# A two-engine weight-sum pipeline in the down projection of a hybrid decoder layer: two of four block sums formed on VectorE, dead storage reused, steps in another order

## The chip, the cores and the metric

One Trainium2 (trn2) chip, one of its cores. The metric is the device time of one execution of the whole program in microseconds (us), as the median of several runs. The profiled execution has a trace of its own; every instruction time below comes from it.

## The reference

The kernel computes one decoder layer on 256 tokens behind 16 prepended meta tokens, 2048 features wide, in float32. All that matters here is the last part, the gated feed-forward block with a causal convolution over three tokens:

```python
u = rmsnorm(h, norm_ffn)
up = causal_dwconv(u @ w_up, ffn_conv_w, ffn_conv_b)
gate, val = jnp.split(up, [FFN_DIM], axis=-1)      # FFN_DIM = 5632
h = h + (jax.nn.silu(gate) * val) @ w_down         # w_down: 5632 x 2048
h = rmsnorm(h, norm_final)                         # the last 256 rows are the output
```

Ahead of it stand the input projection, eight retention heads, four mLSTM heads and the output projection, which the change does not touch.

## The kernel before, in words

All products are made in float32 precision out of a faster format (`F32R`): each operand x is split into hi = x rounded to that format and lo = x - hi, and a product is hi*hi + hi*lo + lo*hi, three matmuls. A weight tile arrives by DMA in a home called `wraw` (four homes, also used by all other weights), ScalarE copies it to `whi` (five homes), VectorE subtracts to give `wlo` (five homes), and TensorE multiplies. A weight tile is 128 x 1024 floats, 512 KB.

The feed-forward block runs in two halves of the 5632 features. In each half an up phase computes 22 tiles of gate and value (`conv3`, silu, product) and stores the results split, and a down phase multiplies them with the half's rows of `w_down` and adds to the residual `hn` (two token blocks `tt` of 128 rows, 2048 columns). The first half is `half` 0, the second `half` 1. A helper `norm2` in the first up phase uses a scratch tile `tb` as well, and so do the sums of activations in the up phase (L720 to L724).

The down phase goes over two pairs of column blocks of 512, `b` = 0 and 2, so the pair is (b, b + 1). For each it walks 11 steps `q` of 256 features (two rows of blocks of 128):

- An even step (`PLAIN`) loads the two weight tiles of the pair with `load_step` and calls `product` for both token blocks: 24 matmuls of 512 columns.
- An odd step (`FAST`, function `seven`) treats 2 token blocks x 2 feature blocks times 2 feature blocks x 2 column blocks as a 2 x 2 product made with seven block products in place of eight: 21 matmuls. It needs the weight tiles `raw0` and `raw1` themselves and four sums of their blocks: GpSimd (POOL in the profile) forms them, two in `ta`, two in `tb`, in a chain: ta1 = raw1[1] - raw1[0], tb0 = ta1 + raw0[0], ta0 = raw1[0] - raw0[0], tb1 = raw0[1] - tb0 (L757). `raw0` uses a `wraw` home; `raw1`, `ta` and `tb` have one home each. Each of the four is then split (L696 on ScalarE, L697 on VectorE) and multiplied (L771, L772, L775), in the order raw0, raw1, ta, tb: 6, 3, 6 and 6 matmuls.

Four accumulators `cs[tt, j]` (PSUM name `atps`) hold what belongs to one output block, four others `ps` (`mmps`) what several output blocks share. After the last odd step `share` folds the shared ones into `hn` with one ScalarE copy and eight VectorE additions, keeping its running sum in the first half of `ta` (L780). After the last step `add` (L798) adds each `cs` to `hn`. In half 1 `squares` (ScalarE) and `times_gain` (POOL, L644) follow at once on each finished block for the final norm. The very last column block, 3, has its even steps in a tail behind the loop of the last pair, with two token blocks staggered by `lag` = 4 steps, so that `finish` of token block 0 lies beside the last matmuls.

Each engine has a queue that runs in the order in which the compiler's scheduler wrote it; the scheduler goes by program order among what it believes to be ready. SyncE (SP) issues the weight loads from one queue, in order. `hT` is the residual in transposed form, 128 x 16 x 272 floats; its last readers are the transposes (L622) that fill `hn` in the first up phase, after which it is dead but keeps its home to the end.

Of the kernel before, what the change touches and what calls it, by code (L numbers as in the profile page):

```python
# [10 lines left out]
F32 = mybir.dt.float32  # L11
# [5 lines left out]
P = 128  # L17
# [66 lines left out]
def trunk(ctx: ExitStack, tc: tile.TileContext, io, out: bass.AP):  # L84
    nc = tc.nc

    def pool(name, bufs, **kw):
        return tc.tile_pool(name=name, bufs=bufs, **kw)
# [515 lines left out]
    def norm2():  # L604
        ms2 = at.tile([P, 512], F32, name="atps")
        nc.tensor.matmul(ms2[:, :NQ], inv_dm, ssq, start=True, stop=True)
        r0, rt = midp.tile([P, 2, 512], F32, name="tb").rearrange("p a t -> a p t")
        r = rsqrt_m2(r0, rt, ms2[:, :NQ], NQ, squared)
        nc.vector.tensor_scalar(out=rstd2, in0=r[:, :NQ], scalar1=-0.5, scalar2=None, op0=ALU.mult)

# [75 lines left out]
    FAST = list(range(1, NQD, 2))  # L686
    PLAIN = list(range(0, NQD, 2))
    S1, S2, S3, S4, A11, A12, A22 = range(7)
    for half in range(2):
        mh = midp.tile([P, 2 * len(PLAIN), SEQ], F32R, name="mh")  # L690
        ml = midp.tile([P, 2 * len(PLAIN), SEQ], F32R, name="ml")
# [7 lines left out]
        for jj in range(NHF):  # L699
            j = half * NHF + jj  # L700
            pair = []
            for s in range(2):
                pair.append(project(io["wu"][2 * j + s], uh, ul, 0))
                if j == 0 and s == 0:
                    norm2()
            gt = conv3(pair[0], j, "gt")
            vt = conv3(pair[1], NF + j, "vt")
            nc.scalar.activation(gt, gt, AF.Silu)
            nc.vector.tensor_tensor(out=gt, in0=gt, in1=vt, op=ALU.mult)
            q, i = divmod(jj, 2)  # L710
            if q in PLAIN:
                k = 2 * PLAIN.index(q) + i
                copied, parted = split(mh[:, k, :], ml[:, k, :], gt)
            elif i == 0:
                f = FAST.index(q)
                even = gt
                copied, parted = split(sh[:, f, A11, :], sl[:, f, A11, :], gt[:, 0:P])
            else:
                a11, a21, a12, a22 = even[:, 0:P], even[:, P:], gt[:, 0:P], gt[:, P:]
                sums = midp.tile([P, 2, 512], F32, name="tb")[:, 0, :].rearrange("p (a t) -> p a t", a=4)  # L720
                nc.gpsimd.tensor_tensor(out=sums[:, S1, :], in0=a21, in1=a22, op=ALU.add)
                nc.gpsimd.tensor_tensor(out=sums[:, S3, :], in0=a11, in1=a21, op=ALU.subtract)  # L722
                nc.gpsimd.tensor_tensor(out=sums[:, S2, :], in0=sums[:, S1, :], in1=a11, op=ALU.subtract)
                nc.gpsimd.tensor_tensor(out=sums[:, S4, :], in0=a12, in1=sums[:, S2, :], op=ALU.subtract)  # L724
                split(sh[:, f, A12:, :], sl[:, f, A12:, :], gt.rearrange("p (a t) -> p a t", a=2))
                copied, parted = split(sh[:, f, 0:4, :], sl[:, f, 0:4, :], sums)
            if 2 <= j < 18:
                with tc.issue_after(parted.ins):
                    transposed_h((j - 2) // 4, (j - 2) % 4)
# [12 lines left out]
            for i in range(2):  # L742
                nc.tensor.matmul(ps, mh[:, k + i, rows], lo[:, i, cols], start=False, stop=last and i == 1)  # L743

        def seven(w0, w1, q, cs, ps, fresh):

            f = FAST.index(q)
            raw0 = wpool.tile([P, 2, 512], F32, name="wraw", bufs=4)
            nc.sync.dma_start(raw0, w0)
            raw1 = midp.tile([P, 2, 512], F32, name="raw1")  # L750
            nc.sync.dma_start(raw1, w1)

            ta, tb = (midp.tile([P, 2, 512], F32, name=n) for n in ("ta", "tb"))
            sums = ((ta, 1, raw1[:, 1, :], raw1[:, 0, :], ALU.subtract), (tb, 0, ta[:, 1, :], raw0[:, 0, :], ALU.add),
                    (ta, 0, raw1[:, 0, :], raw0[:, 0, :], ALU.subtract), (tb, 1, raw0[:, 1, :], tb[:, 0, :], ALU.subtract))
            for t, i, a, b, op in sums:
                nc.gpsimd.tensor_tensor(out=t[:, i, :], in0=a, in1=b, op=op)  # L757
            first, last = q == FAST[0], q == FAST[-1]
            for w, to in (
                (raw0, ((A11, ps[0], first, last), (A12, cs[0, 0], False, False))),  # L760
                (raw1, (None, (S4, cs[0, 1], first and fresh, False))),
                (ta, ((S1, ps[1], first, last), (S3, ps[2], first, last))),
                (tb, ((S2, ps[3], first, last), (A22, cs[1, 0], False, False))),
            ):
                hi = wpool.tile([P, 2, 512], F32R, name="whi", bufs=5)
                lo = wpool.tile([P, 2, 512], F32R, name="wlo", bufs=5)
                a = 1 if to[0] is None else 0
                split(hi[:, a:, :], lo[:, a:, :], w[:, a:, :])
                for i in range(a, 2):
                    m, o, begin, _ = to[i]  # L770
                    nc.tensor.matmul(o, sh[:, f, m, :], hi[:, i, :], start=begin, stop=False)  # L771
                    nc.tensor.matmul(o, sl[:, f, m, :], hi[:, i, :], start=False, stop=False)  # L772
                for i in range(a, 2):
                    m, o, _, end = to[i]
                    nc.tensor.matmul(o, sh[:, f, m, :], lo[:, i, :], start=False, stop=end)  # L775

        def share(ps, b):

            p1, p5, p7, p6 = ps
            x = midp.tile([P, 2, 512], F32, name="ta")[:, 0, :]  # L780
            h = lambda tt, j: hn[:, tt, (b + j) * 512 : (b + j + 1) * 512]

            def plus(o, a, c):
                nc.vector.tensor_tensor(out=o, in0=a, in1=c, op=ALU.add)

            nc.scalar.copy(x, p1)
            plus(h(0, 0), p1, h(0, 0))
            plus(x, p6, x)
            plus(h(0, 1), p5, h(0, 1))
            plus(h(0, 1), x, h(0, 1))  # L790
            plus(x, p7, x)
            plus(h(1, 0), x, h(1, 0))
            plus(x, p5, x)
            plus(h(1, 1), x, h(1, 1))

        def add(ps, tt, c0):
            h = hn[:, tt, c0 : c0 + ps.shape[1]]
            nc.vector.tensor_tensor(out=h, in0=ps, in1=h, op=ALU.add)  # L798

        if half == 1:  # L800
            wk2_cm.__exit__(None, None, None)
            up_cm.__exit__(None, None, None)
            more_cm = pool("more", 3, side="right")
            more = more_cm.__enter__()
            gfin = more.tile([P, DM], F32, name="gfin", bufs=1)
            nc.gpsimd.dma_start(gfin, io["gfin"])
            junk = more.tile([P, 512], F32, name="junk", bufs=1)

        def load_step(b, q, to=wpool):
            return load_w(io["wd"][b, half * NQD + q], [P, 2, 512], to)  # L810

        for b in (0, 2):
            cs = {}
            for j in range(2):
                for tt in range(2):
                    cs[tt, j] = at.tile([P, 512], F32, name="atps")
            ps = [mm.tile([P, 512], F32, name="mmps") for _ in range(4)]

            final = half == 1 and b == 2
            for q in range(NQD):  # L820
                if q in FAST:
                    seven(io["wd"][b, half * NQD + q], io["wd"][b + 1, half * NQD + q], q, cs, ps, final)
                    if q == FAST[-1]:
                        share(ps, b)
                    continue
                for j in range(1 if final else 2):
                    w = load_step(b + j, q)
                    for tt in range(2):
                        product(cs[tt, j], tt, q, w, q == PLAIN[0], q == PLAIN[-1])
            for j in range(1 if final else 2):  # L830
                for tt in range(2):
                    c = (b + j) * 512
                    add(cs[tt, j], tt, c)
                    if half == 1:
                        squares(tt, b + j, c, c + 512)
                        times_gain(tt, c, c + 512)


        if half == 1:
            lag = 4  # L840
            c = 3 * 512
            ws = {}
            for n, q in enumerate(PLAIN):
                ws[q] = load_step(3, q, more if n % 2 else wpool)
                product(cs[0, 1], 0, q, ws[q], False, q == PLAIN[-1])
                if n >= lag:
                    q = PLAIN[n - lag]
                    product(cs[1, 1], 1, q, ws.pop(q), q == PLAIN[0], q == PLAIN[-1 - lag])
            add(cs[0, 1], 0, c)
            squares(0, 3, c, DM)  # L850
            gather(0, 3)
# [96 lines left out]
```

## Time and profile before

| what | us |
|---|---|
| median of three runs | 1245.96 (1245.83 to 1246.23) |
| the profiled execution | 1246.28 |
| its span, first to last instruction | 1244.5 |
| TensorE busy | 1217.1 (98%) |
| VectorE busy | 943.1 (76%) |
| ScalarE busy | 690.1 (55%) |
| POOL busy | 233.6 (19%) |
| first down phase, from its first to its last matmul | 720.66 to 845.30 |
| second down phase, first pair | 1099.44 to 1157.80 |
| second down phase, last pair with the tail | 1157.80 to 1236.05 |

The 1.8 us between the profiled execution and its span lie around the first and the last instruction. Matmuls overlap in their records, so the pace of TensorE is read from start to start, not from the durations. DVE is VectorE, ACT is ScalarE, PE is TensorE, PEld its weight loads, SP is SyncE. An entry `ta<-raw` is an instruction that writes a tile `ta` and reads `raw`; `raw` there is `raw1`, as the digits of names are left out.

### The profile page before, as it was taken

The numbers are of one execution on the slowest core, as the hardware profiler recorded it, in microseconds if no ns is written. First come the engines' busy times: TensorE is split into PE (matmuls) and PEld (weight loads), VectorE is DVE, ScalarE is ACT, GpSimd is POOL, SyncE is SP. The second block draws the span as 40 slices with busy tenths as digits, with TensorE's granted clock in tenths as the row PEclk, the third lists the DMA queues.
The fourth block names the chain that finished last, engine by engine and source line by source line (L and its number), as shares of the span: only waits on it lengthen the run. The fifth ranks groups of instructions, "written<-read, shape, count | busy, mean of one in ns | idle before, by whom it ended". The sixth has DMA issues, their size and how long they took to land.

```text
span 1244.5 us, 22568 instructions
## 1 busy us (share of the span) xinstructions
PE 1217.1 (98%) x8974; PEld 1160.6 (93%) x8974; DVE 943.1 (76%) x1349; ACT 690.1 (55%) x933; POOL 233.6 (19%) x183
## 2 busy tenths in 40 slices
PE   9999999999999999999999999899999999999787
PEld 9999999999999999999999987679999999988566
DVE  8877778677666667888888786879777777787776
ACT  8747655665557556555555545445555555554443
POOL 0100000111001110000100254460100100136661
PEclk9999999999999999999999999999999999999798
DMA  7765555655664655555555545557655555555343
GB/s 273 268 204 168 173 185 171 200 164 185 190 190 150 199 182 199 184 184 177 185 186 180 177 153 183 167 178 249 188 185 176 183 186 185 182 188 172 120 154 134
DMA packets 73290, 228.91 MB, mean 184 GB/s; under 512 B 13408, under 2 KB 17632, under 8 KB 73056
## 3 DMA queue, kind: packets, MB, share of 16 engines
q1 hardware_dynamic: 71952, 223.85, 54.9%
q0 software_dynamic: 656, 2.76, 0.7%
q8 instruction: 70, 1.15, 0.4%
q10 hardware_dynamic: 576, 0.85, 0.2%
q14 instruction: 36, 0.29, 0.1%
HBM read 222.98 MB, written 4.46 MB: 183 GB/s over the span
## 4 chain that ended last, share of the span: by engine, by line
PE 89%; POOL 3%; DVE 3%; DMA 2%; issue 2%; ACT 1%; SPq 0%; DVEq 0%; POOLq 0%; ACTq 0%
PE mmps L137 25%; PE mmps L140 25%; PE mmps L138 25%; PE atps L740 2%; PE atps L741 2%; PE atps L743 2%; POOL tb L757 2%; DMA raw<-in_wd 2%; DVE wlo L697 1%; POOL ta L757 1%; PE mmps L771 1%; PE mmps L775 1%; PE mmps L772 1%; PE atps L775 1%; PE atps L772 1%
## 5 line engine op out<-in xcount | busy, mean ns | idle before, releaser
L128 ACT CAST whi<-wraw 128x1024 fp32r<-128x1024 f32 x364 | 380.5, 1050 | 340.9 <-PE mmps L138 249.4
L130 DVE TENSOR_TENSOR wlo<-wraw,whi 128x1024 fp32r<-128x1024 f32 x364 | 461.5, 1271 | 71.1 <-ACT whi L128 66.9
L138 PE MATMUL mmps<-ul,whi 128*128 128x258 f32 x1408 | 345.8, 283 | 0.0
L137 PE MATMUL mmps<-uh,whi 128*128 128x258 f32 x1408 | 345.5, 282 | 0.0
L137 PEld LDWEIGHTS mmps<-uh,whi 128*128 128x128 f32 x1408 | 266.1, 189 | 0.1
L138 PEld LDWEIGHTS mmps<-ul,whi 128*128 128x128 f32 x1408 | 265.1, 188 | 0.1
L137 PE MATMUL mmps<-xh,whi 128*128 128x272 f32 (+2 forms) x864 | 220.2, 288 | 0.0
L138 PE MATMUL mmps<-xl,whi 128*128 128x272 f32 (+2 forms) x864 | 218.9, 286 | 0.0
L140 PE MATMUL mmps<-uh,wlo 128*128 128x258 f32 x1408 | 198.9, 284 | 0.0
L140 PEld LDWEIGHTS mmps<-uh,wlo 128*128 128x128 f32 x1408 | 182.4, 189 | 0.0
L137 PEld LDWEIGHTS mmps<-xh,whi 128*128 128x128 f32 x864 | 162.9, 189 | 0.1
L138 PEld LDWEIGHTS mmps<-xl,whi 128*128 128x128 f32 x864 | 162.6, 188 | 0.0
L140 PE MATMUL mmps<-xh,wlo 128*128 128x272 f32 (+2 forms) x864 | 127.1, 286 | 0.0
L140 PEld LDWEIGHTS mmps<-xh,wlo 128*128 128x128 f32 x864 | 114.7, 188 | 0.0
L626 DVE TENSOR_TENSOR cu<-mmps,rstd 128x258 f32<-128x258 f32 x88 | 37.5, 426 | 84.7 <-PE mmps L140 84.3
L740 PE MATMUL atps<-whi,mh 128*128 128x512 f32 (+1 forms) x200 | 78.9, 396 | 1.2 <-DVE hn L798 1.2
L741 PE MATMUL atps<-whi,ml 128*128 128x512 f32 (+1 forms) x200 | 78.2, 393 | 0.0
L722 POOL TENSOR_TENSOR tb<-gt 128x128 f32<-128x128 f32 x10 | 14.0, 1403 | 312.0 <-ACT whi L128 282.1
L138 PE MATMUL mmps<-mixl,whi 128*128 128x258 f32 x256 | 63.1, 283 | 0.0
L137 PE MATMUL mmps<-mixh,whi 128*128 128x258 f32 x256 | 62.5, 283 | 0.0
L743 PE MATMUL atps<-wlo,mh 128*128 128x512 f32 (+1 forms) x200 | 59.6, 386 | 0.0
L757 POOL TENSOR_TENSOR ta<-raw 128x512 f32<-128x512 f32 x20 | 33.6, 1680 | 119.0 <-DMA raw<-in_wd 75.0
(254 smaller groups left out, 1705.7 us busy)
## 6 DMA issues: line engine op xcount, KB each, us to landing
wraw<-in_wu SPq DMA_DIRECT2D x176, 512.0 KB, 3.5
wraw<-in_wi SPq DMA_DIRECT2D x108, 512.0 KB, 4.2
wraw<-in_wd SPq DMA_DIRECT2D x68, 512.0 KB, 3.6
wraw<-in_wo SPq DMA_DIRECT2D x32, 512.0 KB, 3.6
raw<-in_wd SPq DMA_DIRECT2D x20, 512.0 KB, 4.3
wraw<-in_w SPq DMA_DIRECT2D x7, 320.0 KB, 5.3
hT<-in_xT SPq DMA_DIRECT2D x7, 272.0 KB, 5.7
e<-in_decay POOLq DMA_DIRECT2D x8, 209.0 KB, 3.1
```

The source lines that it names most:

```text
L128: nc.scalar.copy(hi, raw)
L130: nc.vector.tensor_tensor(out=lo, in0=raw, in1=hi.bitcast(F32), op=ALU.subtract)
L137: nc.tensor.matmul(ps, hi[:, k, :], xh(kk), start=kk == first, stop=False)
L138: nc.tensor.matmul(ps, hi[:, k, :], xl(kk), start=False, stop=False)
L140: nc.tensor.matmul(ps, lo[:, k, :], xh(kk), start=False, stop=kk == last)
L626: nc.vector.tensor_tensor(out=u, in0=ps[:, :NQ], in1=rstd2, op=ALU.mult)
L740: nc.tensor.matmul(ps, mh[:, k + i, rows], hi[:, i, cols], start=first and i == 0, stop=False)
L741: nc.tensor.matmul(ps, ml[:, k + i, rows], hi[:, i, cols], start=False, stop=False)
L743: nc.tensor.matmul(ps, mh[:, k + i, rows], lo[:, i, cols], start=False, stop=last and i == 1)
L757: nc.gpsimd.tensor_tensor(out=t[:, i, :], in0=a, in1=b, op=op)
L772: nc.tensor.matmul(o, sl[:, f, m, :], hi[:, i, :], start=False, stop=False)
L775: nc.tensor.matmul(o, sh[:, f, m, :], lo[:, i, :], start=False, stop=end)
```

## The change

Five things, all in the feed-forward block:

1. VectorE forms ta0 = raw1[1] - raw1[0] and ta1 = ta0 + raw0[0]; POOL forms only tb0 = raw1[0] - raw0[0] and tb1 = raw0[1] - ta1. (The blocks have changed places inside `ta` and `tb`, and with them the order of the products.)
2. The 4096 first floats of a row of the dead `hT` are cut in four homes: two for `raw1`, used in turn, one each for `ta` and `tb`. The tiles `raw1`, `ta`, `tb` of before are gone; three tiles `x0` to `x2` of half their size take their place, for `norm2`, the activation sums and `share`. `raw1` is now loaded ahead of `raw0`.
3. `share` leaves three running sums in `x0` to `x2` and adds to `hn` only what belongs to the two blocks that need one shared accumulator: five VectorE additions. At the end of the pair, VectorE adds `cs` to the running sum and POOL adds that to `hn`. In the last pair the running sums are added to `hn` directly, one on VectorE, two on POOL.
4. The steps run in the order 0, 2, 1, 4, 3, 6, 5, 8, 7, 9, 10.
5. In the last pair, the even steps 0 and 2 do both column blocks in the loop; the tail does only the last four for block 3. Its own pool of weight tiles has two homes in place of three.

```diff
-        r0, rt = midp.tile([P, 2, 512], F32, name="tb").rearrange("p a t -> a p t")
+        r0, rt = (midp.tile([P, 512], F32, name=f"x{i}") for i in range(2))
...
+    left = hT.rearrange("p k t -> p (k t)")[:, 0:4096].rearrange("p (i a n) -> i p a n", i=4, a=2)
+    turn = 0
...
             raw0 = wpool.tile([P, 2, 512], F32, name="wraw", bufs=4)
-            nc.sync.dma_start(raw0, w0)
-            raw1 = midp.tile([P, 2, 512], F32, name="raw1")
-            nc.sync.dma_start(raw1, w1)
-
-            ta, tb = (midp.tile([P, 2, 512], F32, name=n) for n in ("ta", "tb"))
-            sums = ((ta, 1, raw1[:, 1, :], raw1[:, 0, :], ALU.subtract), (tb, 0, ta[:, 1, :], raw0[:, 0, :], ALU.add),
-                    (ta, 0, raw1[:, 0, :], raw0[:, 0, :], ALU.subtract), (tb, 1, raw0[:, 1, :], tb[:, 0, :], ALU.subtract))
-            for t, i, a, b, op in sums:
-                nc.gpsimd.tensor_tensor(out=t[:, i, :], in0=a, in1=b, op=op)
+            raw1, ta, tb = left[turn], left[2], left[3]
+            turn = 1 - turn
+            nc.sync.dma_start(raw1, io["wd"][b + 1, half * NQD + q])
+            nc.sync.dma_start(raw0, io["wd"][b, half * NQD + q])
+
+            nc.vector.tensor_tensor(out=ta[:, 0, :], in0=raw1[:, 1, :], in1=raw1[:, 0, :], op=ALU.subtract)
+            nc.vector.tensor_tensor(out=ta[:, 1, :], in0=ta[:, 0, :], in1=raw0[:, 0, :], op=ALU.add)
+            nc.gpsimd.tensor_tensor(out=tb[:, 0, :], in0=raw1[:, 0, :], in1=raw0[:, 0, :], op=ALU.subtract)
+            nc.gpsimd.tensor_tensor(out=tb[:, 1, :], in0=raw0[:, 1, :], in1=ta[:, 1, :], op=ALU.subtract)
...
-            p1, p5, p7, p6 = ps
-            x = midp.tile([P, 2, 512], F32, name="ta")[:, 0, :]
...
-            nc.scalar.copy(x, p1)
-            plus(h(0, 0), p1, h(0, 0))
-            plus(x, p6, x)
-            plus(h(0, 1), p5, h(0, 1))
-            plus(h(0, 1), x, h(0, 1))
-            plus(x, p7, x)
-            plus(h(1, 0), x, h(1, 0))
-            plus(x, p5, x)
-            plus(h(1, 1), x, h(1, 1))
+            p1, p7, p6, p5 = ps
+            x6, x7, x5 = (x_tile(i) for i in range(3))
+            nc.scalar.copy(x6, p1)
+            plus(block(0, b), p1, block(0, b))
+            plus(x6, p6, x6)
+            plus(x7, p7, x6)
+            plus(block(0, b + 1), p5, block(0, b + 1))
+            plus(x5, p5, x7)
+            return {(0, 1): x6, (1, 0): x7, (1, 1): x5}
...
-            for q in range(NQD):
+            steps = [0, 2, 1, 4, 3, 6, 5, 8, 7, 9, 10]
...
-                for j in range(1 if final else 2):
+                for j in range(2):
+                    if final and j == 1 and q in PLAIN[-lag:]:
+                        continue
...
-                    add(cs[tt, j], tt, c)
-                    if half == 1:
+                    if final:
+                        if (tt, j) in xs:
+                            plus(block(tt, b + j), xs[tt, j], block(tt, b + j), nc.gpsimd if j else None)
+                        if j == 0:
+                            add(cs[tt, j], tt, c)
+                    elif (tt, j) in xs:
+                        plus(xs[tt, j], cs[tt, j], xs[tt, j])
+                        plus(block(tt, b + j), xs[tt, j], block(tt, b + j), nc.gpsimd)
+                    else:
+                        add(cs[tt, j], tt, c)
+                    if half == 1 and not (final and j == 1):
                         squares(tt, b + j, c, c + 512)
                         times_gain(tt, c, c + 512)
```

More of the change, by code (lines that the diff above doesn't have):

```diff
@@ L688, in trunk, with x_tile @@
     S1, S2, S3, S4, A11, A12, A22 = range(7)
+    left = hT.rearrange("p k t -> p (k t)")[:, 0:4096].rearrange("p (i a n) -> i p a n", i=4, a=2)
+    turn = 0
+    def x_tile(i):
+        return midp.tile([P, 512], F32, name=f"x{i}")
     for half in range(2):
@@ L719, in trunk @@
                 a11, a21, a12, a22 = even[:, 0:P], even[:, P:], gt[:, 0:P], gt[:, P:]
-                sums = midp.tile([P, 2, 512], F32, name="tb")[:, 0, :].rearrange("p (a t) -> p a t", a=4)
+                sums = x_tile(0).rearrange("p (a t) -> p a t", a=4)
                 nc.gpsimd.tensor_tensor(out=sums[:, S1, :], in0=a21, in1=a22, op=ALU.add)
@@ L743, in product, with seven @@
                 nc.tensor.matmul(ps, mh[:, k + i, rows], lo[:, i, cols], start=False, stop=last and i == 1)
-        def seven(w0, w1, q, cs, ps, fresh):
+        def seven(b, q, cs, ps, first, last, fresh):
+            nonlocal turn
             f = FAST.index(q)
             raw0 = wpool.tile([P, 2, 512], F32, name="wraw", bufs=4)
-            nc.sync.dma_start(raw0, w0)
-            raw1 = midp.tile([P, 2, 512], F32, name="raw1")
-            nc.sync.dma_start(raw1, w1)
-            ta, tb = (midp.tile([P, 2, 512], F32, name=n) for n in ("ta", "tb"))
-            sums = ((ta, 1, raw1[:, 1, :], raw1[:, 0, :], ALU.subtract), (tb, 0, ta[:, 1, :], raw0[:, 0, :], ALU.add),
-                    (ta, 0, raw1[:, 0, :], raw0[:, 0, :], ALU.subtract), (tb, 1, raw0[:, 1, :], tb[:, 0, :], ALU.subtract))
-            for t, i, a, b, op in sums:
-                nc.gpsimd.tensor_tensor(out=t[:, i, :], in0=a, in1=b, op=op)
-            first, last = q == FAST[0], q == FAST[-1]
+            raw1, ta, tb = left[turn], left[2], left[3]
[6 more added lines that the diff above has]
+            nc.gpsimd.tensor_tensor(out=tb[:, 1, :], in0=raw0[:, 1, :], in1=ta[:, 1, :], op=ALU.subtract)
             for w, to in (
                 (raw0, ((A11, ps[0], first, last), (A12, cs[0, 0], False, False))),
-                (raw1, (None, (S4, cs[0, 1], first and fresh, False))),
-                (ta, ((S1, ps[1], first, last), (S3, ps[2], first, last))),
-                (tb, ((S2, ps[3], first, last), (A22, cs[1, 0], False, False))),
+                (raw1, (None, (S4, cs[0, 1], fresh, False))),
+                (ta, ((S3, ps[1], first, last), (S2, ps[2], first, last))),
+                (tb, ((S1, ps[3], first, last), (A22, cs[1, 0], False, False))),
             ):
@@ L775, in seven, with plus, block @@
                     nc.tensor.matmul(o, sh[:, f, m, :], lo[:, i, :], start=False, stop=end)
+        def plus(o, a, c, engine=None):
+            (engine or nc.vector).tensor_tensor(out=o, in0=a, in1=c, op=ALU.add)
+        def block(tt, b):
+            return hn[:, tt, b * 512 : (b + 1) * 512]
         def share(ps, b):
-            p1, p5, p7, p6 = ps
-            x = midp.tile([P, 2, 512], F32, name="ta")[:, 0, :]
-            h = lambda tt, j: hn[:, tt, (b + j) * 512 : (b + j + 1) * 512]
-            def plus(o, a, c):
-                nc.vector.tensor_tensor(out=o, in0=a, in1=c, op=ALU.add)
-            nc.scalar.copy(x, p1)
-            plus(h(0, 0), p1, h(0, 0))
-            plus(x, p6, x)
-            plus(h(0, 1), p5, h(0, 1))
-            plus(h(0, 1), x, h(0, 1))
-            plus(x, p7, x)
-            plus(h(1, 0), x, h(1, 0))
-            plus(x, p5, x)
-            plus(h(1, 1), x, h(1, 1))
+            p1, p7, p6, p5 = ps
[7 more added lines that the diff above has]
+            return {(0, 1): x6, (1, 0): x7, (1, 1): x5}
         def add(ps, tt, c0):
@@ L802, in trunk @@
             up_cm.__exit__(None, None, None)
-            more_cm = pool("more", 3, side="right")
+            more_cm = pool("more", 2, side="right")
             more = more_cm.__enter__()
@@ L810, in load_step @@
             return load_w(io["wd"][b, half * NQD + q], [P, 2, 512], to)
+        lag = 4
         for b in (0, 2):
@@ L819, in trunk @@
             final = half == 1 and b == 2
-            for q in range(NQD):
+            steps = [0, 2, 1, 4, 3, 6, 5, 8, 7, 9, 10]
+            fast = [q for q in steps if q in FAST]
+            for q in steps:
                 if q in FAST:
-                    seven(io["wd"][b, half * NQD + q], io["wd"][b + 1, half * NQD + q], q, cs, ps, final)
-                    if q == FAST[-1]:
-                        share(ps, b)
+                    seven(b, q, cs, ps, q == fast[0], q == fast[-1], False)
+                    if q == fast[-1]:
+                        xs = share(ps, b)
                     continue
-                for j in range(1 if final else 2):
+                for j in range(2):
+                    if final and j == 1 and q in PLAIN[-lag:]:
+                        continue
                     w = load_step(b + j, q)
                     for tt in range(2):
-                        product(cs[tt, j], tt, q, w, q == PLAIN[0], q == PLAIN[-1])
-            for j in range(1 if final else 2):
+                        product(cs[tt, j], tt, q, w, q == PLAIN[0], q == PLAIN[-1 - (lag if final and (tt, j) == (1, 1) else 0)])
+            for j in range(2):
                 for tt in range(2):
                     c = (b + j) * 512
-                    add(cs[tt, j], tt, c)
-                    if half == 1:
+                    if final:
[9 more added lines that the diff above has]
+                    if half == 1 and not (final and j == 1):
                         squares(tt, b + j, c, c + 512)
@@ L839, in trunk @@
         if half == 1:
-            lag = 4
             c = 3 * 512
             ws = {}
-            for n, q in enumerate(PLAIN):
+            for n, q in enumerate(PLAIN[-lag:]):
                 ws[q] = load_step(3, q, more if n % 2 else wpool)
                 product(cs[0, 1], 0, q, ws[q], False, q == PLAIN[-1])
-                if n >= lag:
-                    q = PLAIN[n - lag]
-                    product(cs[1, 1], 1, q, ws.pop(q), q == PLAIN[0], q == PLAIN[-1 - lag])
             add(cs[0, 1], 0, c)
```

## The prediction

> **What bounds the kernel now.** I read the page first (TensorE is busy all the time), then TensorE's pace against the number of matmuls of each stage, then who keeps it waiting, then what that one waits for.
>
> ```profile
> PE 1217.1 (98%) x8974; PEld 1160.6 (93%) x8974; DVE 943.1 (76%) x1349; ACT 690.1 (55%) x933; POOL 233.6 (19%) x183
> 720.66 0.39 PE L740 MATMUL atps<-whi,mh 128*128 128x512 f32 x1
> 722.06 0.40 PE L740 MATMUL atps<-whi,mh 128*128 128x512 f32 x1
> 720.66:845.30 124.64, 119.32 (x500) 92.34 (x499) 96.09 (x82) 60.22 (x67) 66.36 (x36) 1.00 0.52 174
> 1099.44:1157.80 58.36, 58.36 (x253) 46.96 (x252) 46.79 (x40) 31.07 (x35) 29.53 (x17) 1.00 0.58 196
> 1157.80:1236.05 78.25, 65.83 (x273) 50.70 (x271) 57.67 (x61) 34.66 (x49) 42.94 (x27) 0.89 0.36 121
> 1236.05:1244.50 8.45, 0.17 (x2) 0.00 (x0) 2.56 (x8) 1.73 (x5) 0.00 (x0) 0.62 0.40 146
> ```
>
> Six matmuls of 512 columns lie between the two starts 720.66 and 722.06, so TensorE's pace is 0.233 us. A pair of column blocks has 6 x 24 + 5 x 21 = 249 of them, 58.1 us. The first down phase (two pairs) should take 116.2 us and takes 124.6: 8.4 lost. The first pair of the second loses 0.3, the last pair with the tail 78.25 - 58.1 = 20.1 (its granted clock is 0.89). That is 28.8 us in all that this change can win; the 8.45 us behind the last matmul stay.
>
> ```profile
> PE mmps L771 <- ACT whi L696: 14.5, 9, 4.2
> ACT whi L696 <- POOL tb L757: 40.2, 14, 6.1
> POOL ta L757 <- DMA raw<-in_wd: 75.0, 14, 10.8
> 748.00 4.42 DMA raw<-in_wd
> 752.59 1.80 issue
> 754.39 1.74 POOL ta L757
> 756.13 1.26 POOL tb L757
> 757.46 2.17 POOL tb L757
> 760.08 4.37 DMA raw<-in_wd
> ```
>
> The first three rows are waits (total, times, longest): TensorE waits for a split in an odd step, ScalarE's split for POOL's sums, POOL for the load of `raw1`. The others, from the chain, are one turn of that circle: `raw1` has one home, so its next load starts when POOL is through, and a turn takes 760.08 - 748.00 = 12.1 us, where TensorE needs 45 x 0.233 = 10.5 for an even and an odd step. That is the first limit. The second is a queue between VectorE and POOL:
>
> ```profile
> 749.79 2.35 DVE L130 TENSOR_TENSOR wlo<-wraw,whi 128x1024 fp32r<-128x1024 f32 x2
> 752.06 1.22 DVE L697 TENSOR_TENSOR wlo<-wraw,whi 128x1024 fp32r<-128x1024 f32 x1
> 1162.14 0.68 DVE L798 TENSOR_TENSOR hn<-atps,hn 128x512 f32<-128x512 f32 x1
> 1162.74 0.68 DVE L784 TENSOR_TENSOR hn<-ta,hn 128x512 f32<-128x512 f32 x1
> 788.43 1.30 POOL L757 TENSOR_TENSOR ta<-raw,wraw 128x512 f32<-128x512 f32 x1
> 789.69 1.28 POOL L757 TENSOR_TENSOR tb<-ta,wraw 128x512 f32<-128x512 f32 x1
> 1174.32 2.29 POOL L757 TENSOR_TENSOR ta<-raw,wraw 128x512 f32<-128x512 f32 x1
> 1175.39 2.31 DVE L130 TENSOR_TENSOR wlo<-wraw,whi 128x1024 fp32r<-128x1024 f32 x1
> 1177.62 2.30 DVE L697 TENSOR_TENSOR wlo<-wraw,whi 128x1024 fp32r<-128x1024 f32 x1
> 1159.67 1.29 POOL L644 TENSOR_TENSOR hn<-hn,gfin 128x512 f32<-128x512 f32 x1 [11.32 <-ACT junk L640]
> ```
>
> Start to start, a VectorE split of 1024 columns takes 1.13 us alone and 512 columns take 0.60; a POOL sum alone 1.26. Side by side they take turns: VectorE's split then takes 2.23 (1175.39 to 1177.62), so each POOL sum costs VectorE 1.1. POOL's gain at 1159.67 ran at its lone pace beside VectorE additions from PSUM; those don't take turns.
>
> **The change part by part.**
>
> *The sums.* An odd step now costs VectorE, with POOL's turns, 3 x 1.13 + 0.60 (splits) + 4 x 1.1 = 8.4 us; a whole pair 12 x 1.13 + 5 x 8.4 + 3 x 0.6 (additions out of `ta`) = 57.4, and 9 additions from PSUM at 0.6, 5.4: 62.8. The first down phase took 62.3 a pair, so these prices hold. Afterwards an odd step costs 3 x 1.13 + 0.60 + 2 x 0.60 + 2 x 1.1 = 7.4. A pair: 13.6 + 37 + 3 x 1.1 for POOL's new additions = 53.9, and 9 PSUM additions 5.4 (before, 12 in all): 59.3 against TensorE's 58.1, with 5.4 that may run beside POOL. So it loses 0 to 1.2 a pair. I take the middle: 1.3 for the first down phase where it lost 8.4. Ends: nothing lost, or all 8.4 still there.
>
> *The homes.* With two homes for `raw1` the 12.1 us circle opens: the load of step f waits for the readers of step f-2. What is late next is `tb`, still one home: two sums beside splits (2.29 at worst each), ScalarE's copy, VectorE's split:
>
> ```profile
> 1166.04 1.04 ACT L696 CAST whi<-ta 128x1024 fp32r<-128x1024 f32 x1 [0.89 <-POOL ta L757]
> 679.28 1.30 DVE L622 STREAM_TRANSPOSE hn<-hT 32x512 f32<-32x512 f32 x2
> POOL tb L722 <- ACT whi L128: 282.1, 9, 32.2
> ```
>
> 2 x 2.3 + 1.04 + 1.23 = 6.9 us a turn. That is within 10.5, but not within the 21 x 0.233 = 4.9 of step 7, behind which 9 now follows directly: 2.0 late unless the splits are 2.0 ahead. The even step 8 ahead of it gives them 5.6 us of matmuls for two splits (2.3), so I cost it at nothing; without that cover, 2.0 a pair, 8 in all. `raw1` and `raw0` exchange places in SP's queue: equal counts of loads, and the one that waited (`raw1`) now rarely does, so nothing behind it is later. The first load into `hT` can't go before the transposes (the last at 679.28), 41 us ahead of the first down phase; the same load went early before, so nothing. `x0`, `x1` for `norm2` and the activation sums: POOL pauses there for up to 32.2 us at a time; nothing.
>
> *Share.* Five VectorE additions where there were eight and a free `ta`: the next pair's sums needn't wait for it. POOL's additions come on top of `times_gain` in half 1. New waits: POOL's addition waits for VectorE's, and behind it on POOL stand the gains and tb of the next pair's step 1; VectorE's ta sums wait for `raw1`'s load, and behind them stand the splits of the step. TensorE waits for both through the splits.
>
> *The last pair*, where the most was lost.
>
> ```profile
> 1165.96 3.51 POOL L644 TENSOR_TENSOR hn<-hn,gfin 128x512 f32<-128x512 f32 x2
> 1167.13 0.79 PE L771 MATMUL mmps<-whi,sh 128*128 128x512 f32 x1 [3.22 <-ACT whi L696]
> 1168.15 0.63 PE L771 MATMUL mmps<-whi,sh 128*128 128x512 f32 x1
> 1168.58 0.63 PE L772 MATMUL mmps<-whi,sl 128*128 128x512 f32 x1
> 1169.44 1.26 POOL L757 TENSOR_TENSOR tb<-ta,wraw 128x512 f32<-128x512 f32 x1
> 1174.27 0.79 PE L771 MATMUL mmps<-whi,sh 128*128 128x512 f32 x1 [4.21 <-ACT whi L696]
> 1211.00:1213.00 2.00, 0.80 (x3) 0.30 (x2) 2.00 (x2) 0.77 (x1) 1.20 (x1) 1.00 0.00 0
> 1214.50:1218.00 3.50, 3.50 (x10) 2.75 (x10) 3.50 (x6) 2.20 (x3) 0.00 (x0) 0.55 0.94 305
> ```
>
> POOL's gains (1165.96) stood between the sums of step 1, TensorE stood still for 3.22 and 4.21 us, and its pace behind it was 0.43 (1168.15 to 1168.58). Its even steps do one block only, 12 matmuls, 2.8 us. Old order: tb of the last odd step is wanted 5 x 2.8 + 4 x 4.9 + 3.5 (15 matmuls of its own step) = 37.1 us after the pair's start; VectorE with POOL's turns needs 5 x 8.4 + 4 x 1.13 + 4 gains x 1.1 + 1.8 = 52.7. That is 15.6 late, near the 20.1 measured, of which about 28 matmuls at 0.43 make 28 x 0.2 = 5.6. New order: wanted at 2 x 5.6 + 3 x 2.8 + 4 x 4.9 + 3.5 = 42.7; needed 5 x 7.4 + 5 x 1.13 + (4 gains + 3 additions) x 1.1 = 50.4, less what the free `ta` and `raw1` allow ahead of the pair, ta's sums and tb0, 2.3: 5.4 late. To that I add one spell at half clock as the last row shows it (eight matmuls, 1.6): 7.0 lost where it was 20.1. Ends: nothing, if gains and additions fall into the tail, and 15.6, if nothing is won.
>
> The half clock deserves a look. The row at 1211 shows TensorE busy 0.80 of 2.00 us, in stalls of under 2 us, and the clock is down at 1214.5 all the same. The Trainium skill (TensorE: Matmul & The Clock Gate, Part 1) says that the clock halves after an idle window of some 3.4 us; by that rule my short stalls would cost no clock, and the estimate would be 1.6 lower. Here the row differs from the page, so I keep the row.
>
> *The tail and all else*: as many matmuls, as many loads, one weight home less for two tiles less. Nothing; behind the last matmul the same 8.45.
>
> The sum: lost before 8.4 + 0.3 + 20.1 = 28.8; after 1.3 + 0.3 + 7.0 = 8.6; won 20.2. The profiled execution, 1246.28 (span 1244.5 and 1.8 around it), becomes 1226.1; the median of the runs stood 0.3 below it: 1225.8, say 1226.
>
> **The rivals.**
>
> *All hidden.* The splits stay ahead, gains and additions slip into gaps, and only some 0.6 us are lost: 1246 - 28 = 1218. For it: the first pair of the second half lost 0.3 only, even with the old prices. Against: it started with step 1's sums made in the up phase; the last pair can't.
>
> *POOL late.* The seven POOL instructions between the pairs go ahead of step 1's tb, and 7 next to 9 costs 2.0 in each pair: 8 us, and a second spell at half clock 1.6: 1226 + 9.6 = 1236. For it: the rows at 1165.96 and 1169.44. Against: tb of step 1 is now wanted 2 x 5.6 + 3.5 = 14.7 us into the pair, in place of 2.8 + 3.5 = 6.3. On the pair's queue the Trainium skill (SBUF — State Buffer, SBUF: two separate sides) has a stricter rule: the one that starts first holds the shared port for the whole instruction and the other fully blocks. By that rule each POOL instruction would cost VectorE its full 1.26 and not 1.1: 0.16 x (10 + 7) = 2.7 more in the last pair, an estimate of 1229.
>
> *No effect.* The load of `raw1` stays as late as now, because SP's queue stands behind other loads, and POOL's wait of 75.0 only changes its name: 1246.
>
> *Slower: VectorE waits where POOL waited.* POOL could wait for `raw1` with nothing behind it; VectorE, when a ta sum stands at the head of its queue, holds up all splits. It decides from (62.3 - 59.3) / 5 = 0.6 us of such waiting in each odd step; with 2.0 us it is 59.3 + 10 = 69.3 a pair, 7 more than now, 28 over four: 1274. The pauses of POOL at the same spot (75.0 in 14, 5.4 each) speak for it, the second home against it: the load has a step's 10.5 us more for its 4.4.
>
> **How the numbers follow.** The measurement tells 0.2% (2.5 us) from no change. Forecast 0.54 (own range 1221 to 1232), all hidden 0.14, POOL late 0.18, no effect 0.04, slower 0.10. Faster: the first three, 0.86; same 0.04; slower 0.10. Leaving out the last two, the range goes from all hidden to POOL late with the stricter port: 1218 to 1238.
>
> **What would show it.** Right: `raw` no longer ends VectorE's or POOL's waits in the chain of the down phases; they take about 118, 58 and 65 us; a pause of TensorE is under 3 us; POOL shows 40 fewer sums and 11 more additions. The sums are mis-priced if VectorE's 512-column sums take far from 0.60 start to start, or POOL's turns cost more than 1.1. Wrong at the root: VectorE rows with a pause that ends on `raw`'s load, or loads of `raw1` that still wait for POOL.

## The result, and the profile after

| | us | ratio to before, 95% interval |
|---|---|---|
| before, median of five runs | 1245.95 | |
| after, median of five runs | 1225.91 | 0.9841 [0.9827, 0.9856] |
| after, profiled execution | 1225.65 (span 1223.9) | |

The change won 20.0 us. The page of the changed kernel first, its engine row and the shares of its chain, then the same four stretches as before (first down phase; first pair and last pair of the second; what lies behind the last matmul), then TensorE's waits (total, times, longest).

```profile
PE 1208.3 (99%) x8974; PEld 1157.8 (95%) x8974; DVE 964.7 (79%) x1378; ACT 692.9 (57%) x933; POOL 189.6 (15%) x154
PE 94%; DVE 2%; POOL 2%; issue 1%; ACT 0%; DMA 0%; DVEq 0%; ACTq 0%; SPq 0%
```

```profile
720.32:837.11 116.79, 116.44 (x501) 93.40 (x499) 107.19 (x100) 62.25 (x68) 38.87 (x21) 1.00 0.56 190
1091.16:1149.62 58.46, 58.26 (x251) 46.57 (x250) 50.59 (x51) 33.19 (x37) 13.87 (x10) 1.00 0.60 206
1149.62:1214.09 64.47, 60.34 (x273) 47.18 (x273) 62.20 (x59) 31.58 (x46) 39.32 (x21) 1.00 0.34 115
1214.09:1223.90 9.81, 0.04 (x1) 0.00 (x0) 4.17 (x14) 2.65 (x8) 1.07 (x1) 0.70 0.58 215
```

```profile
PE mmps L778 <- ACT whi L703: 2.0, 1, 2.0
PE atps L750 <- DVE wlo L130: 1.4, 2, 0.9
PE mmps L782 <- DVE wlo L704: 0.8, 1, 0.8
PE atps L747 <- DVE hn L804: 0.6, 2, 0.4
```

At 0.233 us a matmul the stretches now lose 116.79 - 116.2 = 0.6, 58.46 - 58.1 = 0.4 and 64.47 - 58.1 = 6.4 us, where they lost 8.4, 0.3 and 20.1. The granted clock is full in all three; before it was 0.89 in the last. TensorE's wait for ScalarE's splits in odd steps (14.5 us in nine) is down to one wait of 2.0 us. One thing got worse: 9.81 us behind the last matmul, where it was 8.45. POOL's 154 instructions are 29 fewer: 40 sums gone, 11 additions new.

What is left stands in the last pair. Its rows on VectorE, POOL and TensorE:

```profile
1155.10 5.88 DVE L704 TENSOR_TENSOR wlo<-hT,whi 128x512 fp32r<-128x512 f32 x3 [0.36 <-PE atps L750]
1155.91 6.23 POOL L785 TENSOR_TENSOR hn<-x,hn 128x512 f32<-128x512 f32 x3
1191.76 1.66 DVE L763 TENSOR_TENSOR hT<-hT,wraw 128x512 f32<-128x512 f32 x1
1194.67 2.33 DVE L704 TENSOR_TENSOR wlo<-wraw,whi 128x1024 fp32r<-128x1024 f32 x1
1194.49 0.50 PE L778 MATMUL mmps<-whi,sh 128*128 128x512 f32 x1 [1.95 <-ACT whi L703]
```

Three splits that take 1.13 each or less alone take 5.88 beside POOL's three new additions, 6.23: they take turns, as before. VectorE is busy 62.2 of 64.47 us there. At 1194.49, the start of step 9, TensorE has its longest pause, 1.95.

### The profile page after: what moved, and what is told of

Read it like the earlier page. It is cut to its first block, busy times and chain, and to the rows that moved or that the text cites. A ratio compares the mean times of both kernels' runs of the same rounds, so it can differ in the third digit from the quotient of the medians.

```text
span 1223.9 us, 22571 instructions
## 1 busy us (share of the span) xinstructions
PE 1208.3 (99%) x8974; PEld 1157.8 (95%) x8974; DVE 964.7 (79%) x1378; ACT 692.9 (57%) x933; POOL 189.6 (15%) x154
## 3 DMA queue, kind: packets, MB, share of 16 engines
q8 instruction: 70, 1.15, 0.4%
## 4 chain that ended last, share of the span: by engine, by line
PE 94%; DVE 2%; POOL 2%; issue 1%; ACT 0%; DMA 0%; DVEq 0%; ACTq 0%; SPq 0%
PE mmps L137 25%; PE mmps L140 25%; PE mmps L138 25%; PE atps L750 3%; PE atps L747 3%; PE atps L748 3%; PE mmps L778 1%; PE mmps L779 1%; PE mmps L782 1%; PE atps L778 1%; PE atps L779 1%; PE atps L782 1%; DVE wlo L130 1%; POOL hn L785 1%; POOL hn L644 1%
## 5 line engine op out<-in xcount | busy, mean ns | idle before, releaser
L703 ACT CAST whi<-hT 128x1024 fp32r<-128x1024 f32 (+1 forms) x60 | 54.3, 908 | 55.3 <-PE atps L748 23.4
L704 DVE TENSOR_TENSOR wlo<-hT,whi 128x1024 fp32r<-128x1024 f32 (+1 forms) x60 | 71.6, 1225 | 5.5 <-ACT whi L703 4.4
L729 POOL TENSOR_TENSOR x<-gt 128x128 f32<-128x128 f32 x10 | 15.1, 1509 | 321.5 <-ACT whi L128 257.6
```

The costliest lines, as they stand in the source:

```text
L703: copied = nc.scalar.copy(hi, x)
L704: return copied, nc.vector.tensor_tensor(out=lo, in0=x, in1=hi.bitcast(F32), op=ALU.subtract)
```

## The experiments

Each kernel was run four to six times, in turn with the kernel before on the same chip; times are medians. "Lost" is always a stretch less 116.2 or 58.1 us, from its trace. The theory behind the forecast was that VectorE with POOL's turns sets the pace; its rival, that the one home of `raw1` did.

**Homes alone, on the kernel before.** Only this was added to it:

```diff
-            raw1 = midp.tile([P, 2, 512], F32, name="raw1")
+            raw1 = left[turn]
+            turn = 1 - turn
```

> The kernel before with two homes for raw1 in the dead residual, and nothing else changed: sums on POOL, old order, old share. Theory (VectorE's turns with POOL): a pair still needs 62.8 us, so little is won, 0 to 4 us: 1242 to 1246. Rival (the 12.1 us circle was the limit): the 1.6 us lost in each odd step come back, 6 us in the first down phase and about 8 in the last pair: 1232 to 1236.

Measured: 1234.62 us, 0.9907 [0.9894, 0.9920]. Its first down phase, first pair and last pair:

```profile
720.60:838.98 118.38, 116.90 (x501) 92.94 (x499) 108.11 (x83) 60.91 (x67) 70.20 (x36) 1.00 0.56 183
1093.04:1151.14 58.10, 58.10 (x252) 46.74 (x251) 53.16 (x44) 32.44 (x37) 32.00 (x18) 1.00 0.60 200
1151.14:1224.60 73.46, 63.50 (x274) 48.42 (x272) 62.44 (x58) 33.70 (x47) 46.63 (x27) 0.93 0.35 115
```

The rival was right for the first down phase: 6.2 of its 8.4 lost us come back with all four sums still on POOL. The last pair keeps 15.4 of its 20.1. So there are two limits, and each rules another stretch, though the last pair gets 4.7 back from the homes too.

**The sums on VectorE alone, on the kernel before** (its first two, with everything else old):

```diff
-                nc.gpsimd.tensor_tensor(out=t[:, i, :], in0=a, in1=b, op=op)
+                (nc.vector if (t is ta) == (i == 1) else nc.gpsimd).tensor_tensor(out=t[:, i, :], in0=a, in1=b, op=op)
```

> The kernel before with the first two sums of its chain (ta1 and tb0) on VectorE and nothing else changed: one home for raw1, old order, old share. Theory of turns: an odd step costs 7.4 and not 8.4, and the circle through raw1's home shrinks from 12.1 to about 9: 8 to 12 us faster than before, 1234 to 1238. Rival (VectorE waits at the head of its queue for raw1, as the kernel with one home showed, 39 us in 18 waits): no gain or slower, 1246 to 1256.

Measured: 1253.18 us, 1.0062 [1.0041, 1.0082]: slower than before. A row of its waits, its first down phase, and the first and the last pair of the second:

```profile
DVE ta L757 <- DMA raw<-in_wd: 35.4, 14, 4.7
720.87:852.23 131.36, 121.26 (x500) 94.99 (x499) 110.01 (x104) 62.49 (x69) 33.41 (x18) 0.97 0.53 171
1106.29:1170.96 64.67, 59.15 (x251) 46.44 (x250) 51.62 (x50) 31.91 (x36) 15.41 (x9) 1.00 0.55 179
1170.96:1243.00 72.04, 63.45 (x274) 49.04 (x272) 63.96 (x69) 34.17 (x49) 28.29 (x17) 0.93 0.38 126
```

The turns became fewer and the last pair lost less (13.9 where it was 20.1), but VectorE now stands 14 times, 35.4 us in all, for the load that POOL used to wait for, the first down phase loses 15.2 where it lost 8.4, and the first pair of the second 6.6 where it lost 0.3.

**Both, with share, order and last pair as before** (the two edits above together):

> The kernel before with both parts put in together: two homes for raw1 in the dead residual, and the first two sums of the chain on VectorE; old order, old share in ta, old last pair. Theory (the two parts need each other and carry the change): homes alone won 11, the sums alone lost 8, together the first down phase loses nothing and the last pair about 10 (share still lends ta, gains in front of tb): 1229 to 1232. Rival (share and the last pair's edits carry nothing): 1223, as the changed kernel in the old order. Second rival (they carry most): 1236 or above.

Measured: 1228.38 us, 0.9865 [0.9848, 0.9881].

```profile
721.58:838.81 117.23, 116.74 (x500) 93.33 (x499) 110.42 (x104) 62.81 (x68) 32.28 (x18) 1.00 0.60 191
1150.97:1219.00 68.03, 61.29 (x274) 48.94 (x272) 63.22 (x68) 33.67 (x47) 29.32 (x17) 0.95 0.41 127
```

Homes won 0.93% by themselves, the sums lost 0.62%, together they win 1.35%: more than their sum of 0.31%. The first down phase is nearly clean. The last pair still loses 9.9, with a pause of 3.15 us at step 1.

**The changed kernel with one home:**

```diff
-            raw1, ta, tb = left[turn], left[2], left[3]
+            raw1, ta, tb = left[0], left[2], left[3]
```

> The changed kernel with a single home for raw1 (left[0] in every odd step); all else as changed. Theory (VectorE's turns): the circle shrinks anyway, since only ta0, tb0 and the split read raw1: load 4.4, 1.8 until the first sum, 2.3 for ta0 and tb0, about 8.5 to 9 us and below the 10.5 of a step pair; 0 to 3 us slower, 1226 to 1229. Rival (homes were what mattered): the circle still rules wherever two odd steps are close, and 8 us or more come back, 1234 or above.

Measured: 1256.91 us, 1.0088 [1.0075, 1.0101]: 31 us over the changed kernel, and slower than before. Its row of VectorE's waits, one of TensorE's, one turn of the load (SP issues it, POOL's and VectorE's first reader), its first down phase, and last, from the changed kernel, the only load that VectorE still waits for in the down phases:

```profile
DVE hT L762 <- DMA hT<-in_wd: 39.1, 18, 4.6
PE atps L750 <- DVE wlo L130: 9.4, 4, 2.6
737.09 1.81 DVE L704 TENSOR_TENSOR wlo<-hT,whi 128x512 fp32r<-128x512 f32 x2
737.80 0.33 SPq L759 DMA_DIRECT2D hT<-in_wd  x1
744.53 1.30 POOL L764 TENSOR_TENSOR hT<-hT,wraw 128x512 f32<-128x512 f32 x1 [9.58 <-DMA hT<-in_wd]
744.82 1.56 DVE L762 TENSOR_TENSOR hT<-hT 128x512 f32<-128x512 f32 x1 [3.45 <-DMA hT<-in_wd]
720.38:855.59 135.21, 123.96 (x501) 96.28 (x499) 106.64 (x99) 62.70 (x68) 40.08 (x21) 0.95 0.51 163
DVE hT L763 <- DMA wraw<-in_wd: 4.4, 6, 1.3
```

The load goes out behind the split of `raw1` (737.09) and its data are used 6.7 us later; VectorE waits 3.45 of that, and what follows in its queue waits with it. My estimate of a harmless 8.5 to 9 us circle missed that a wait on VectorE delays the splits of the even steps too: TensorE's wait for those is 9.4 us (1.4 in the changed kernel), and 19.0 us are lost where it was 8.4. In the changed kernel the row `DVE hT L762 <- DMA` does not appear; what is left are six short waits for the load of `raw0`, 4.4 us in all.

**One home and the order 0 to 10,** to see whether the neighbours 7 and 9 made it so dear:

> The changed kernel with one home for raw1 and the steps in the order 0 to 10. Theory A (the one home is dear only where steps 7 and 9 follow each other): the 31 us that one home cost fall to 3 to 8 us over the old order with two homes (1223.1): 1226 to 1231. Theory B (VectorE waits for raw1 in every odd step): 2.2 us in each of 18, 20 us or more over it, 1243 or above.

Measured: 1261.12 us, 1.0121 [1.0107, 1.0135]. VectorE waits longer still:

```profile
DVE hT L762 <- DMA hT<-in_wd: 51.7, 17, 4.3
```

Theory A fell. The waiting is in nearly every odd step (17 waits in 20), and the new order made it cheaper by some 4 us, not dearer.

**The order, with two homes:**

```diff
-            steps = [0, 2, 1, 4, 3, 6, 5, 8, 7, 9, 10]
+            steps = list(range(NQD))
```

> The changed kernel with the steps in the order 0, 1, 2, ... 10. Theory (VectorE's total up to the last odd step decides, and that is wanted at 42.7 us in either order): the stall of the last pair moves to its beginning but keeps its size, plus some half clock; 0 to 4 us slower, 1226 to 1230. Rival (the order is what gives the start of a pair its cover): each of the four pairs loses 2 us or more at step 1, 8 us or more, 1234 or above.

Measured: 1223.07 us, 0.9815 [0.9802, 0.9828], some 3 us faster than the changed kernel. First down phase and last pair:

```profile
720.55:836.74 116.19, 116.19 (x500) 93.48 (x499) 108.73 (x102) 63.49 (x68) 41.70 (x21) 1.00 0.60 192
1148.89:1211.70 62.81, 59.88 (x274) 47.34 (x272) 60.98 (x60) 32.54 (x46) 37.14 (x20) 1.00 0.38 124
```

Neither theory said this: with the second home the new order costs. Nothing is lost in the first three pairs (1.0 in the changed kernel), and the last loses 4.7 in place of 6.4. The pause in front of step 9 is gone. The two kernels were run in different sessions and their intervals just touch; the stretches say the same. The kernel with homes and sums alone (1228.38) has the same order and differs from this one in share, drain and last pair, in the order of the loads and in which two of the sums are VectorE's: 5.3 us; which edit of that group did it was not separated.

**All four sums back on POOL,** in the changed kernel (its two `nc.vector` sums to `nc.gpsimd`):

> The changed kernel with all four weight sums on POOL again; homes, order, share as changed. Theory (VectorE's time with POOL's turns is the limit): an odd step costs 8.4 us and not 7.4, a pair 64.3 against TensorE's 58.1, the last odd step of the last pair is 5 us later; some 10 us slower than the changed kernel, about 1236. Rival (the 12.1 us circle through the one home of raw1 was the limit, and two homes opened it): within 2 us of the changed kernel, 1226 to 1228.

Measured: 1238.54 us, 0.9936 [0.9924, 0.9949]. First down phase and last pair:

```profile
720.63:842.05 121.42, 118.26 (x501) 94.47 (x500) 103.46 (x81) 61.85 (x67) 76.98 (x40) 0.99 0.54 179
1156.93:1227.80 70.87, 62.84 (x273) 48.08 (x273) 57.42 (x52) 32.09 (x47) 54.63 (x30) 0.98 0.35 108
```

12.6 us back, near what the theory of turns had (about 10): 5.2 lost in the first down phase, 2.7 in the first pair of the second (1096.11 to 1156.93), 12.8 in the last pair. The last pair fits the theory. The first down phase takes 121.42 / 2 = 60.7 a pair and not the 64.3 that it gives; and homes alone, with as many sums on POOL, lost 2.2 there, so the 5.2 don't come from the sums alone. Half of the 5.2 is a single pause of 2.57 in front of the second pair, where TensorE waits for VectorE's addition out of an accumulator (the last section shows it).

**All four on VectorE** (tb's two to `nc.vector`):

> The changed kernel with all four weight sums on VectorE, none on POOL. Theory (turns): an odd step costs 6.4 us and not 7.4, the last pair is through 5 us earlier, so its 6.2 lost shrink to about 1.5: 1221. Rival (VectorE in order is the limit and POOL's sums lie in its pauses): 1.2 us more VectorE work in each odd step, 6 a pair, the last pair loses more: 1228 to 1235.

Measured: 1220.48 us, 0.9794 [0.9782, 0.9807].

```profile
720.85:837.04 116.19, 116.19 (x501) 93.48 (x499) 104.59 (x120) 63.40 (x69) 6.84 (x3) 1.00 0.59 197
1149.20:1209.80 60.60, 59.08 (x274) 47.69 (x272) 58.61 (x73) 32.39 (x48) 21.15 (x12) 1.00 0.38 122
```

The first down phase is clean and the last pair loses 2.5. VectorE does ten more sums a pair and is busy for less time, in the last pair 58.61 us where it was 62.20.

**The additions on VectorE** (`plus` without POOL):

> The changed kernel with the additions of the running sums to hn on VectorE in place of POOL. Theory (POOL's instruction costs VectorE 1.1 in turns, its own 0.6): 1.5 us less VectorE time a pair, the last pair loses 4.5 in place of 6.2, and the end, where an addition by POOL was waited for, is 1.4 shorter: 1223. Rival (VectorE's queue is the tighter one, POOL's turns fit into pauses): the three additions delay splits, 1227 to 1229.

Measured: 1225.62 us, 0.9838 [0.9826, 0.9851]: no difference that counts.

```profile
1149.33:1212.80 63.47, 60.21 (x274) 47.19 (x273) 62.13 (x62) 31.31 (x45) 27.51 (x16) 1.00 0.37 118
1212.80:1223.30 10.50, 0.14 (x2) 0.00 (x0) 4.95 (x15) 2.86 (x8) 0.94 (x1) 0.72 0.54 201
```

The last pair gains 1.0, the end gives 0.7 back.

**Without the gains on the first pair's columns,** which leaves that part of the final norm out:

> The changed kernel without times_gain on all but the last pair's column block 2 and the tail, so the final gain is left out on the columns of the first pair. Theory (each POOL instruction costs VectorE 1.1 in turns, and the last pair has no room): four fewer, the 6.2 us lost in the last pair become about 2, 1221 to 1222. Rival (gains lie in VectorE's pauses): within 1 us of the changed kernel.

Measured: 1221.47 us, 0.9811 [0.9796, 0.9825]. Its last pair:

```profile
1150.39:1209.80 59.41, 59.03 (x273) 47.65 (x273) 57.29 (x59) 31.66 (x46) 28.97 (x17) 1.00 0.40 127
```

Four POOL instructions fewer, and the last pair loses 1.3 in place of 6.4: 1.3 us each, where no room is left. (This is the price of a gain in whatever way it acts; its place in POOL's own queue was not separated from its turns with VectorE.)

**Two combinations,** the order 0 to 10 with all sums on VectorE, and the additions there too:

> The changed kernel in the order 0 to 10 with all four sums on VectorE. Theory (turns with POOL and the order are separate costs): 1223.1 for the old order, less the 5 that the last two sums won, and no less than the 1217.5 that remain when nothing is lost: 1218 to 1219. Rival (both cure the same stall): 1220 to 1221, no better than all sums on VectorE in the changed order (1220.5).

> As the run before, and the additions of the running sums to hn on VectorE too, so that POOL does the gains alone. Theory (a POOL addition costs VectorE 1.1 in turns, its own 0.6): 0 to 1 us faster than with POOL's additions. Rival (in the tail VectorE's queue is what ends last): 0.5 to 2 us slower, all of it behind the last matmul.

Measured: 1220.81 us, 0.9805 [0.9790, 0.9820], and 1219.59 us, 0.9796 [0.9782, 0.9811]. With all sums on VectorE no difference by the order shows (1220.48 in the other; 2.4 and 2.5 lost in the last pair), as the rival had it. The last is the fastest median of all, with 1.4 us lost in its last pair. Its four runs (1219.33 to 1220.20) lie below the four of the kernel measured beside it (1220.52 to 1220.99); from the one of the other session it cannot be told.

## Why the prediction was right

The time came out (1226 forecast, 1225.91 measured), and the mechanism of the last pair, most of the gain, held in the main. Some of its terms missed, and they cancelled; that the sum met the measurement to 0.1 is luck.

- *First down phase.* Forecast 1.3 lost, measured 0.6. But the reason given for the 8.4 before was wrong. The step that failed is "The first down phase took 62.3 a pair, so these prices hold": with homes alone the same number of POOL turns took 118.38 / 2 = 59.2 a pair. The agreement of 62.8 with 62.3 was chance; the circle through `raw1`'s home set that stretch. Not every POOL turn there costs the 1.1; that it does so only where VectorE has work queued at that moment would explain it, but no run shows this by itself.
- *Last pair.* Forecast 7.0 (5.4 late and 1.6 at half clock), measured 6.4, all of it at full clock. Here VectorE is busy throughout and the price of a turn held: 1.3 us for a gain left out. Taking two more sums off POOL in each of five odd steps won 3.9, where their turns' price less VectorE's own, 10 x (1.1 - 0.6), is 5.0. The spell at half clock didn't come, so the 5.4 alone stand against the 6.4. And VectorE's total was not all that made this pair late before: homes alone, which change no term of that sum, took 4.7 off it.
- *The neighbours 7 and 9* were "costed at nothing". They and the new start of a pair cost some 3 us, with a pause of 1.95 in front of step 9 of the last pair. The text had priced 2.0 for the case that the cover fails, but by the one home of `tb`, and this pause came another way, so that the sizes agree is chance:

```profile
1185.95 2.30 DVE L704 TENSOR_TENSOR wlo<-wraw,whi 128x1024 fp32r<-128x1024 f32 x1
1188.32 4.11 DMA wraw<-in_wd
1192.45 1.04 ACT L128 CAST whi<-wraw 128x1024 fp32r<-128x1024 f32 x1 [4.19 <-DMA wraw<-in_wd]
```

VectorE's split of `raw0`, which took 2.30, released its `wraw` home late. The next load into a `wraw` home started right behind it, and ScalarE stood 4.19 us for that tile, an even step's, with the copy of step 9's `raw0` behind it in its queue. The prediction counted the loads and found nothing later; it didn't ask when the `wraw` homes come free.

- *The end* was "nothing" and cost 1.4. The last addition in both kernels, before and after, with the last matmuls of the changed kernel between:

```profile
1236.26 0.42 DVE L798 TENSOR_TENSOR hn<-atps,hn 128x256 f32<-128x256 f32 x1 [1.05 <-PE atps L743]
1213.73 0.40 PE L750 MATMUL atps<-wlo,mh 128*128 128x256 f32 x2
1214.83 0.74 DVE L667 SCALAR_TENSOR_TENSOR hn<-hn,frt,gfin 128x512 f32<-128x512 f32 x1
1215.75 0.41 DVE L804 TENSOR_TENSOR hn<-atps,hn 128x256 f32<-128x256 f32 x1
```

Before, VectorE was idle and waited for TensorE. After, TensorE was through at 1214.1, and the addition stood until 1215.75 behind the scaling of the first token block, which VectorE reached late. With all sums on VectorE, which gets there earlier, the end took 8.70 (1209.80 to 1218.50). The step that failed is the one that counted matmuls and loads of the tail and not VectorE's queue.

- *The rival "slower"* was real, and what the prediction said would prevent it did: with one home the predicted waits of VectorE appeared (2.2 us each in the changed kernel with one home, 18 times, above the 0.6 from which it was to decide), and the kernel was slower than before. With two they are gone, and the 4.4 us for `raw0` are 0.2 an odd step. Its price was right in kind: 1256.9, against the 1274 worked out for 2.0 us.
- *One reading* stood on the wrong row. The gain at 1159.67 overlapped only the end of one addition from PSUM, and VectorE's next addition, out of `ta`, took 1.56 beside it: a turn. Another place in the kernel before bears the reading out, a sum and an addition from PSUM that start together and both take their lone time (the last two rows):

```profile
1159.94 1.56 DVE L784 TENSOR_TENSOR hn<-ta,hn 128x512 f32<-128x512 f32 x1
1163.50 1.28 POOL L757 TENSOR_TENSOR ta<-raw 128x512 f32<-128x512 f32 x1 [2.55 <-DVE hn L784]
1163.53 0.69 DVE L798 TENSOR_TENSOR hn<-atps,hn 128x512 f32<-128x512 f32 x1
```

## What to carry to other kernels

Before work moves from an engine that may wait to one that may not, give the data it will wait for a second home: here the second home alone won 0.9%, the moved sums alone lost 0.6%, and both together won 1.35%. Where VectorE and POOL take turns, an instruction moved off POOL can shorten VectorE's time even if VectorE has to do it; here the kernel gained by it mainly in the last pair, where VectorE is busy throughout; a price is to be checked by a run that changes it, not by a sum that happens to agree. And count the queue of the finishing engine in the tail, not only the matmuls in front of it.

## What the runs showed of the hardware that was not expected

With all sums on POOL, one pause of TensorE of 2.57 us was enough for the clock to halve for 3.4 us:

```profile
781.45 0.47 PE L747 MATMUL atps<-whi,mh 128*128 128x512 f32 x1 [2.57 <-DVE hn L804]
779.20:782.60 3.40, 1.15 (x5) 1.00 (x6) 3.40 (x5) 2.10 (x2) 1.11 (x1) 1.00 0.92 286
782.60:786.00 3.40, 3.40 (x10) 2.62 (x9) 3.40 (x5) 0.00 (x0) 3.40 (x3) 0.50 0.82 278
```

In the 3.4 us ahead of it TensorE was busy 1.15. The changed kernel's pause of 1.95 us at 1194.49 had no such effect. But the length of one pause doesn't decide it. In the kernel before, a spell of the same length came where no pause in the 5 us ahead of it was longer than 1.47 (first three rows below), while the changed kernel kept its clock through 3.40 us in which TensorE was busy less (last row):

```profile
1213.33 0.50 PE L771 MATMUL mmps<-whi,sh 128*128 128x512 f32 x1 [1.47 <-ACT whi L696]
1210.80:1214.20 3.40, 1.87 (x8) 0.97 (x6) 3.37 (x3) 1.97 (x3) 1.40 (x1) 1.00 0.30 52
1214.20:1217.60 3.40, 3.40 (x10) 2.64 (x9) 3.40 (x5) 2.50 (x4) 0.00 (x0) 0.50 0.94 300
1192.60:1196.00 3.40, 1.51 (x6) 1.09 (x7) 3.29 (x3) 3.36 (x5) 2.63 (x2) 1.00 0.11 12
```

The Trainium skill (TensorE: Matmul & The Clock Gate, Part 1) asks for an idle window of about 3.4 us; the length of the spell agrees, the idle time needed was less here. On what the limit depends stays open.
